# A matmul with rotary embedding: all input tiles turned by TensorE as 32-bit words, in place of fp16 transposes and block pairs

## The chip, the core and the metric

The kernel runs on one core of a Trainium2 chip. The metric is the device time in microseconds of one execution, as the median of several runs. The engines are TensorE (PE; its weight loads are listed apart as PEld), VectorE (DVE), ScalarE (ACT), GpSimd (POOL) and SyncE (SP). Transfers are issued from the queues of SP, ACT and POOL and are moved by the core's 16 DMA engines.

## The reference

```python
batch, seq, hidden, n_heads = (16, 512, 768, 12)      # head_dim 64
y = np.matmul(x, weight)                               # x (16, 512, 768), weight (768, 768), fp32
y = y.reshape(batch, seq, n_heads, head_dim)
y1, y2 = y[..., :head_dim // 2], y[..., head_dim // 2:]
...
out1 = y1 * cos1 - y2 * sin1                           # cos, sin (seq, head_dim), halves 1 and 2
out2 = y2 * cos2 + y1 * sin2
out = np.concatenate([out1, out2], axis=-1).reshape(batch, seq, hidden).astype(np.float32)
```

Every row of x is multiplied by the weight, and in the product each head's two halves are rotated with cos and sin of the row's place in its sequence.

## The kernel before

The 8192 rows of x are cut into 64 tiles of 128 rows (`NTILE`), and four tiles make a group (`QB = 4`, 16 groups, `LAST` is 15). A group holds the same quarter of the sequence rows of four batches, so that one slice of cos and sin serves the whole group.

The contraction runs over 768 values of a row. TensorE needs them on partitions, so each tile has to be transposed. The contraction is split in six chunks (`CHUNKS`, a pair t of 0 to 2 and e of 0 or 1): chunk (t, e) holds the values p·6 + 2t + e for partition p. Two neighbouring fp16 values (e = 0 and 1) form one 32-bit word.

**Plain tiles** (44 of 64) go through four steps. `load` (L188) brings 128 rows of fp32 into one of ten buffers `xs`, issued by SP. `cast` (L223) makes fp16 of them on ACT and sorts them by t, m, e into `xc`. `turn` (L231) lets TensorE transpose the six chunks by an fp16 identity (L238) into the PSUM buffer `pt`, one of two. A copy (L240, run through the helper at L172) moves `pt` to `xt`, on DVE for the first two tiles and on ACT for the rest.

**Block pairs** (20 tiles in ten pairs, the second half of each group from 5 to 14) are transposed by no TensorE instruction. `load_quarter` (L196) brings a quarter of the contraction of two tiles onto 32 partitions; four such transfers make a pair. For odd groups SP issues them in fp32 (`xb`) and ACT casts the pair (`cast_pair`, L243, into `xd`). For even groups POOL issues them and they arrive in fp16 (`xh`). `turn_pair` (L251) then lets DVE transpose 32x32 blocks of 32-bit words into `xp` (L263), in which the two values of a word are neighbours; the matmuls read them with a step of two.

**Matmuls.** `mm_piece` (L297) multiplies one chunk of a tile by the weight (`w_sb`, fp16) into a piece of a PSUM ring `py` of six banks. A tile's 768 output columns fall into two pieces, 512 and 256 wide, so that a tile takes twelve matmuls. The turned x is the stationary operand, the weight the moving one.

**After the matmul.** `rope` (L310) takes 1024 columns at once (a unit; smaller ones in the last two groups): DVE multiplies them by cos and by the signed sin into `tq` (L320), and POOL adds the two products into `ov` (L331); the last four adds are on DVE. `store` (L342) writes half a group of rows, mostly from ACT's queue.

**Order.** Each engine runs its instructions in the order in which the program names them; `Flow.do` adds the waits. After the matmuls of tile i the main loop (L522) names the block transposes up to tile i + 6 (`bturns`, `B_AHEAD`), the plain transposes and evictions up to tile i + 3 (`turns`, `T_AHEAD`), the casts up to tile i + 7 (`casts`, `C_AHEAD`; fewer in the first groups), POOL's loads up to 20 tiles ahead (`pool_loads`) and, at the first and third tile of a group, a store of the group before. `pump` names SP's loads in an order made beforehand (`fetch`, L374), as far as the buffers allow: ten `xs` and three `xb`. Before the loop stands an opening, in which the first four tiles are multiplied chunk by chunk as the weight's six parts arrive (`load_w`, `cast_w`, `mm0`), after twelve matmuls on zeros (`warm`).

Of the kernel before, what the change touches and what calls it, by code (L numbers as in the profile page):

```python
# [103 lines left out]
def kernel(  # L104
# [16 lines left out]
    NH = int(n_heads)  # L121
    D = H // NH
    HD = D // 2
    R = 32
    NQ = P // R
    NT = H // (2 * P)
    SB = S // P
    QB = 4
# [3 lines left out]
    LAST = NG - 1  # L132


    BLOCKS = {}
    for g in range(5, 15):
        BLOCKS[g, 1] = "pool" if g % 2 == 0 and g >= 4 else "sp"

    def sbuf(name, shape, dt):
        return nc.alloc_sbuf_tensor(name, shape, dt).ap()  # L140

    NX, NB, NBH, NC, NCP, NXT, NXP, NTQ, NOV = 10, 3, 3, 5, 2, 8, 4, 3, 4

    ident = sbuf("ident", [P, P], FP16)
    cold = sbuf("cold", [P, 512], FP16)
    sin_sb = sbuf("sin_sb", [P, SB, D], FP32)
    csn = sbuf("csn", [P, 2, SB, D], FP32)
    w_raw = sbuf("w_raw", [P, NT, 2, H], FP32)
    w_sb = sbuf("w_sb", [P, NT, 2, H], FP16)
    xs_b = [sbuf(f"xs{i}", [P, H], FP32) for i in range(NX)]  # L150
    xb_b = [sbuf(f"xb{i}", [P, 2 * H], FP32) for i in range(NB)]
    xh_b = [sbuf(f"xh{i}", [P, 2 * H], FP16) for i in range(NBH)]
    xc_b = [sbuf(f"xc{i}", [P, H], FP16) for i in range(NC)]
    xd_b = [sbuf(f"xd{i}", [P, 2 * H], FP16) for i in range(NCP)]
    xt_b = [sbuf(f"xt{i}", [P, NT, 2, P], FP16) for i in range(NXT)]
    xp_b = [sbuf(f"xp{i}", [P, 2 * H], FP16) for i in range(NXP)]
    tq_b = [sbuf(f"tq{i}", [P, 2, 1024], FP32) for i in range(NTQ)]
    w_flat = w_raw.rearrange("p t e n -> p (t e n)")
    tq_b += [w_flat[:, ts(i, 2048)].rearrange("p (j n) -> p j n", j=2) for i in range(2)]
# [5 lines left out]
    def ring(name, n, state={}):  # L165
        k = state.get((id(f), name), 0)
        state[id(f), name] = k + 1
        return k % n

    def copy(e, o, i_):  # L170
        return lambda eng: (
            eng.copy(out=o, in_=i_) if e == "act" else eng.tensor_copy(out=o, in_=i_)  # L172
        )

    def where(i):
        g, s = divmod(i, QB)
        return QB * (g // SB) + s, g % SB

    def pair_of(i):
        return i // QB, (i % QB) // 2  # L180

    def is_block(i):
        return pair_of(i) in BLOCKS

    xs, xc, xT = {}, {}, {}


    def load(i, e="sp"):  # L188
# [3 lines left out]
        do(e, lambda eng: eng.dma_start(  # L192
            out=xs_b[k], in_=x[b].rearrange("(p r) h -> r p h", r=SB)[r]),
            writes=[f"xs{k}"], dma=f"xs{k}")

    def load_quarter(gh, q):  # L196
        g, h = gh
        b, r = where(g * QB + 2 * h)
        e = BLOCKS[gh]
        src = x[b : b + 2].rearrange("b (j a r) (q k) -> r q a (b j) k", r=SB, a=R, q=NQ)  # L200
        if q == 0:
            xs[gh] = ring("xh", NBH) if e == "pool" else ring("xb", NB)
        k = xs[gh]
        name = f"xh{k}" if e == "pool" else f"xb{k}"
        buf = xh_b[k] if e == "pool" else xb_b[k]
        dst = buf.rearrange("p (j k) -> p j k", j=2 * NQ)
        do(e, lambda eng: eng.dma_start(out=dst[ts(q, R)], in_=src[r, q]),  # L207
           writes=[f"{name}q{q}"], dma=name)

    wv = weight.rearrange("(p t e) n -> t e p n", t=NT, e=2)  # L210

# [19 lines left out]
    def turn(i, e):  # L231
        c = xc[i]
        k = ring("pt", 2)
        z = ring("xt", NXT)
        src = xc_b[c].rearrange("p (t m e) -> p t e m", t=NT, e=2)
        pt = pt_b[k].bitcast(FP16)[:, 0:H].rearrange("p (t e m) -> p t e m", t=NT, e=2)
        for t, h in CHUNKS:
            do("pe", lambda eng: eng.transpose(pt[:, t, h, :], src[:, t, h, :], ident),  # L238
               reads=[f"xc{c}", "ident"], writes=[f"pt{k}"], tick=(t, h) == CHUNKS[-1])
        do(e, copy(e, xt_b[z], pt), reads=[f"pt{k}"], writes=[f"xt{z}"])  # L240
        xT[i] = (lambda t, h: xt_b[z][:, t, h, :], f"xt{z}")

    def cast_pair(gh, e="act"):  # L243
        k = xs[gh]
        c = ring("xd", NCP)
        xc[gh] = c
        do(e, copy(e, xd_b[c].rearrange("p (t j e) -> p t j e", t=NT, e=2),
                   xb_b[k].rearrange("p (j t e) -> p t j e", t=NT, e=2)),
           reads=[f"xb{k}q{q}" for q in range(NQ)], writes=[f"xd{c}"])

    def turn_pair(gh):  # L251
        g, h = gh
        z = ring("xp", NXP)
        dst = xp_b[z].bitcast(FP32)
        if BLOCKS[gh] == "pool":
            k = xs[gh]
            src = xh_b[k].bitcast(FP32).rearrange("p (j t) -> p t j", t=NT)
            rd = [f"xh{k}q{q}" for q in range(NQ)]
        else:
            c = xc[gh]  # L260
            src, rd = xd_b[c].bitcast(FP32), [f"xd{c}"]
        v = xp_b[z].rearrange("p (t m e) -> p t e m", t=NT, e=2)
        do("dve", lambda eng: eng.transpose(out=dst, in_=src), reads=rd, writes=[f"xp{z}"])  # L263
        for s in (0, 1):
            xT[g * QB + 2 * h + s] = (
                lambda t, e, s=s: v[:, t, e, ts(s, P)], f"xp{z}")

    def units(g):  # L270
        if g < LAST - 1:
# [99 lines left out]
        out=sin_sb, in_=sin.rearrange("(p r) d -> p r d", r=SB)), writes=["sin"], dma="sin")  # L371


    fetch, quarters = [], []  # L374
    soon = [p for p in sorted(BLOCKS) if BLOCKS[p] == "sp"]
    for i in range(QB, NTILE):
        if soon and i >= max(2, soon[0][0] - 1) * QB:
            quarters += [(soon[0], q) for q in (0, 2, 1, 3)]
            soon.pop(0)
        if not is_block(i):  # L380
            fetch.append(i)
            if quarters:
                fetch.append(quarters.pop(0))
        elif quarters and quarters[0][0] == pair_of(i):
            fetch.append(quarters.pop(0))
    fetched = [0]
    xs_used, xb_used = [0], [0]
    xs_sent, xb_sent = [4], [0]

    def pump():  # L390

        while fetched[0] < len(fetch):
            j = fetch[fetched[0]]
            if isinstance(j, int):
                if xs_sent[0] - xs_used[0] >= NX:
                    return
                load(j)
                xs_sent[0] += 1
            else:
                if j[1] == 0:  # L400
                    if xb_sent[0] - xb_used[0] >= NB:
                        return
                    xb_sent[0] += 1
                load_quarter(*j)
            fetched[0] += 1

    WARM = 12
    warmed = [0]
# [42 lines left out]
    for c in CHUNKS[3:5]:  # L451
# [6 lines left out]
    do("dve", lambda eng: eng.tensor_scalar_mul(  # L458
        out=csn[:, 1, :, HD:D], in0=sin_sb[:, :, 0:HD], scalar1=-1.0),
        reads=["sin", "csn1", "cos"], writes=["csn"])  # L460
    assert not quarters
    pump()

    state = {"cast": 4, "turn": 4, "bturn": 0, "pool": 0}
    pairs = sorted(BLOCKS)
    pool_pairs = [p for p in pairs if BLOCKS[p] == "pool"]

    def casts(upto):
        while state["cast"] < min(upto, NTILE):
            i = state["cast"]  # L470
            state["cast"] += 1
            if not is_block(i):
                castx(i, "act")
            elif i % 2 == 0 and BLOCKS[pair_of(i)] == "sp":
                cast_pair(pair_of(i))
                xb_used[0] += 1
            pump()

    def turns(upto):
        while state["turn"] < min(upto, NTILE):  # L480
            i = state["turn"]
            state["turn"] += 1
            if not is_block(i):
                turn(i, "act")

    def bturns(upto):
        while state["bturn"] < len(pairs):
            gh = pairs[state["bturn"]]
            if gh[0] * QB + 2 * gh[1] >= upto:
                return  # L490
            turn_pair(gh)
            state["bturn"] += 1

    def pool_loads(upto):
        while state["pool"] < len(pool_pairs):
            gh = pool_pairs[state["pool"]]
            if gh[0] * QB + 2 * gh[1] >= upto:
                return
            for q in (0, 2, 1, 3):
                load_quarter(gh, q)  # L500
            state["pool"] += 1

    C_AHEAD, T_AHEAD, B_AHEAD, P_AHEAD = 7, 3, 6, 20
    SETTLED = 2 * QB


# [15 lines left out]
    for i in range(QB, NTILE):  # L522
        g, s = divmod(i, QB)
        us = units(g)
        done_to = (s + 1) * H
        for p in pieces(g, s):
            a, z, _, bank = p
            for c in CHUNKS:
                mm_piece(i, p, c, c == CHUNKS[0], c == CHUNKS[-1],
                         tick=c == CHUNKS[-1])  # L530
            for u in us:
                if u[1] == z:
                    rope(g, u)
        bturns(i + (B_AHEAD if i >= SETTLED else 3))
        turns(i + 1 + (T_AHEAD if i > QB + 1 else 2))
        casts(i + 1 + (C_AHEAD if i >= SETTLED else 3 if i == QB else 4))
        pool_loads(i + P_AHEAD)
        if s == 0 and g > 0:
            store(g - 1, 0, 2 * H, "act")
        if s == 2 and g > 0:  # L540
            store(g - 1, 2 * H, 4 * H, "act")
        if g == LAST:
            if s == 2:
                store(g, 0, H, "sp")
            if s == 3:
                store(g, H, 2 * H, "act")
# [42 lines left out]
```

## Time and profile before

| | |
|---|---|
| Median of 3 runs | 157.07 us (156.81 to 157.47) |
| Profiled execution, its own time | 156.38 us |
| Its span, first to last instruction | 154.6 us |
| Granted TensorE clock, mean | 0.991 |
| PE / DVE / ACT / POOL busy | 145.2 / 125.8 / 77.4 / 123.4 us |
| Matmuls of tiles (L302) | 768 to py (528 from xt, 240 from xp) and 12 to pt |
| TensorE transposes (L238) | 264 |
| DVE block transposes (L263) | 10, of 1246 ns (from xh) and 968 ns (from xd) |
| ACT casts of tiles / of pairs | 44 of 905 ns / 5 of 1603 ns |
| ACT evictions pt to xt | 42 of 800 ns |
| x transfers to landing, median | 16.2 us (xs), 16.5 us (xb), 12.3 us (xh) |
| Bytes moved, packets under 2 KB | 51.16 MB, 13072 of 27548 packets |

The page shows one profiled execution. A group of instructions is given by its line, engine and operation, the tile it writes and the one it reads, the shape, the count, the busy time and the mean duration of one. TensorE's instructions are pipelined: 264 transposes of 219 ns keep it busy for only 21.9 us, so the step from one to the next, and not the duration, says what one costs. Slices are fortieths of the span, 3.9 us each, and their digits are busy tenths. The chain is followed back from the last instruction through whatever released each step.

### The profile page before, as it was taken

To read this page: it belongs to the slowest core of one execution; us is meant where nothing else is said; L and a number is where in the kernel's file an instruction comes from. 1 tells how busy PE (TensorE), PEld (TensorE's weight loads), DVE (VectorE), ACT (ScalarE), POOL (GpSimd) and SP (SyncE) were. 2 spreads that over 40 slices of the span, in tenths; PEclk is the share of its full clock that TensorE was granted. 3 is DMA by queue.
4 is the path that set the end of the run, shared out by engine and by line. 5 is a ranking of instruction groups with operands and counts; after the bars stand their busy time and mean duration, and the time that the engine had idled before them with its cause. 6 is when DMAs were issued, how large, how long until landed. Compare 5 with 4: busy or idle time off the path is not lost.

```text
span 154.6 us, 2609 instructions
## 1 busy us (share of the span) xinstructions
PE 145.2 (94%) x1056; PEld 91.9 (59%) x1056; DVE 125.8 (81%) x82; ACT 77.4 (50%) x92; POOL 123.4 (80%) x79
## 2 busy tenths in 40 slices
PE   6799999999999999999999999999999999999930
PEld 2345566666666666566666666665666666666720
DVE  0436997688777979998999899898999899997990
ACT  3462959699658615744282707452483418243000
POOL 1000599799888999799989999899988886999940
PEclk9999999999999999999999999999999999999996
DMA  4999999999999999999999999999999963443983
GB/s 138 387 408 397 403 399 401 368 342 362 372 344 302 395 350 336 358 381 363 351 332 385 391 347 318 365 405 368 368 368 360 382 251 139 155 179 150 374 336 106
DMA packets 27548, 51.16 MB, mean 331 GB/s; under 512 B 7184, under 2 KB 13072, under 8 KB 27536
## 3 DMA queue, kind: packets, MB, share of 16 engines
q1 hardware_dynamic: 13504, 24.78, 45.7%
q10 hardware_dynamic: 8592, 24.25, 39.9%
q0 software_dynamic: 5440, 1.97, 10.3%
q8 instruction: 8, 0.13, 0.3%
q14 instruction: 4, 0.03, 0.1%
HBM read 27.79 MB, written 25.17 MB: 343 GB/s over the span
## 4 chain that ended last, share of the span: by engine, by line
PE 84%; DVE 4%; DMA 4%; ACT 2%; SPq 1%; issue 1%; DVEq 0%
PE py L302 76%; PE pt L238 9%; DMA w_raw<-in_weight_dram 4%; DVE xs L320 1%; ACT xc L172 1%; DVE tq L320 1%; DVE ov L331 1%; SPq L192 1%; DVE w_raw L320 1%; SPq L214 1%; ACT xt L172 1%; DVE w_sb L172 0%; DVEq L55 0%; SPq L584 0%; SPq L114 0%
## 5 line engine op out<-in xcount | busy, mean ns | idle before, releaser
L302 PE MATMUL py<-w_sb,xt 128*128 128x256 f16 (+1 forms) x528 | 89.9, 323 | 1.4 <-DVE w_sb L172 1.1
L331 POOL TENSOR_TENSOR ov<-tq 128x1024 f32<-128x1024 f32 (+2 forms) x33 | 68.9, 2105 | 21.6 <-DVE tq L320 21.4
L320 DVE TENSOR_TENSOR tq<-py,csn 128x2048 f32<-128x2048 f32 (+2 forms) x33 | 66.4, 2024 | 9.3 <-PE py L302 8.9
L302 PEld LDWEIGHTS py<-w_sb,xt 128*128 128x128 f16 x528 | 50.3, 98 | 32.6 <-DVE w_sb L172 2.8
L172 ACT COPY xt<-pt 128x768 f16<-128x768 f16 x42 | 33.5, 800 | 56.1 <-PE pt L238 56.1
L320 DVE TENSOR_TENSOR w_raw<-py,csn 128x2048 f32<-128x2048 f32 (+1 forms) x20 | 41.4, 2068 | 5.8 <-PE py L302 5.7
L331 POOL TENSOR_TENSOR ov<-w_raw 128x1024 f32<-128x1024 f32 (+1 forms) x20 | 42.8, 2149 | 2.6 <-DVE w_raw L320 2.6
L172 ACT CAST xc<-xs 128x768 f16<-128x768 f32 x44 | 39.2, 905 | 8.6 <-DMA xs<-in_x_dram 8.4
L302 PE MATMUL py<-w_sb,xp 128*128 128x512 f16 (+1 forms) x240 | 42.3, 326 | 0.0
L302 PEld LDWEIGHTS py<-w_sb,xp 128*128 128x128 f16 x240 | 22.6, 98 | 12.9
L238 PE MATMUL pt<-ident,xc 128*128 128x128 f16 x264 | 21.9, 219 | 0.2 <-ACT xc L172 0.2
L238 PEld LDWEIGHTS pt<-ident,xc 128*128 128x128 f16 x264 | 18.0, 98 | 6.8 <-ACT xc L172 2.0
L207 POOL DMA_DIRECT2D xh<-in_x_dram x20 | 11.7, 590 | 0.0
L172 ACT CAST xd<-xb 128x1536 f16<-128x1536 f32 x5 | 8.0, 1603 | 0.0
L263 DVE STREAM_TRANSPOSE xp<-xh 128x768 f32<-128x768 f32 x5 | 6.2, 1246 | 0.0
L172 DVE CAST w_sb<-w_raw 128x768 f16<-128x768 f32 x6 | 3.4, 559 | 3.5 <-DMA w_raw<-in_weight_dram 3.5
L413 PE MATMUL py<-cold 128*128 128x512 f16 x12 | 4.6, 552 | 1.4 <-DVE cold L356 1.4
L172 DVE COPY xt<-pt 128x768 f16<-128x768 f16 x2 | 1.1, 558 | 4.8 <-PE pt L238 4.8
L263 DVE STREAM_TRANSPOSE xp<-xd 128x768 f32<-128x768 f32 x5 | 4.8, 968 | 0.0
L413 PEld LDWEIGHTS py<-cold 128*128 128x128 f16 x12 | 1.4, 131 | 3.4 <-issue 1.9
L172 ACT ACT_TABLE_LOAD x1 | 1.3, 1283 | 0.9 <-SPq L114 0.9
L302 PE MATMUL pt<-w_sb,xt 128*128 128x256 f16 x12 | 1.5, 272 | 0.0
(13 smaller groups left out, 6.8 us busy)
## 6 DMA issues: line engine op xcount, KB each, us to landing
out_dram<-ov ACTq DMA_DIRECT2D x30, 768.0 KB, 8.3
xs<-in_x_dram SPq DMA_DIRECT2D x44, 384.0 KB, 16.2
xb<-in_x_dram SPq DMA_DIRECT2D x20, 192.0 KB, 16.5
w_raw<-in_weight_dram SPq DMA_DIRECT2D x6, 384.0 KB, 6.7
xh<-in_x_dram POOLq DMA_DIRECT2D x20, 96.0 KB, 12.3
out_dram<-ov SPq DMA_DIRECT2D x1, 384.0 KB, 2.8
out_dram<-ov ACTq DMA_DIRECT2D x1, 384.0 KB, 2.5
out_dram<-ov SPq DMA_DIRECT2D x1, 256.0 KB, 2.0
```

The source lines that it names most:

```text
L172: eng.copy(out=o, in_=i_) if e == "act" else eng.tensor_copy(out=o, in_=i_)
L192: do(e, lambda eng: eng.dma_start(out=xs_b[k], in_=x[b].rearrange("(p r) h -> r p h", r=SB)[r]), writes=[f"xs{k}"], dma=f"xs{k}")
L207: do(e, lambda eng: eng.dma_start(out=dst[ts(q, R)], in_=src[r, q]), writes=[f"{name}q{q}"], dma=name)
L214: do(e, lambda eng: eng.dma_start(out=w_raw[:, t, h], in_=wv[t, h]), writes=[f"wr{t}{h}"], dma=f"w{t}{h}")
L238: do("pe", lambda eng: eng.transpose(pt[:, t, h, :], src[:, t, h, :], ident), reads=[f"xc{c}", "ident"], writes=[f"pt{k}"], tick=(t, h) == ...
L263: do("dve", lambda eng: eng.transpose(out=dst, in_=src), reads=rd, writes=[f"xp{z}"])
L302: do("pe", lambda eng: eng.matmul(ps, get(t, h), w_sb[:, t, h, a - s * H : z - s * H], start=start, stop=stop), reads=[key, f"w{t}{h}"], w ...
L320: do("dve", lambda eng: eng.tensor_tensor(out=tq.rearrange("p j (h d) -> p j h d", d=D), in0=ps.rearrange("p (h d) -> p h d", d=D) .unsque ...
L331: do(adder, lambda eng: eng.tensor_tensor(out=ov_b[o][:, ds(c0, w)].rearrange("p (h t d) -> p h t d", t=2, d=HD), in0=tq[:, 0].rearrange(" ...
L413: do("pe", lambda eng: eng.matmul(py[:, ts(b, 512)], cold[:, 0:P], cold, start=True, stop=warmed[0] < WARM - 6), reads=["cold"], writes=[f ...
```

## The change

The block pairs go, with their buffers (`xb`, `xh`, `xd`, `xp`), their transfers, casts and DVE transposes. All 64 tiles take the way of a plain tile. In `turn`, TensorE transposes the fp16 tile as fp32 words, three 128x128 transposes per tile in place of six, with an fp32 identity; the copy out of PSUM still moves 768 fp16 values, and the matmuls read them with a step of two. The freed space goes to buffers: 18 `xs` in place of 10, 6 `xc` for 5, 4 `tq` for 3. Casts run five tiles ahead instead of seven.

```diff
-    BLOCKS = {}
-    for g in range(5, 15):
-        BLOCKS[g, 1] = "pool" if g % 2 == 0 and g >= 4 else "sp"
...
-    NX, NB, NBH, NC, NCP, NXT, NXP, NTQ, NOV = 10, 3, 3, 5, 2, 8, 4, 3, 4
-
-    ident = sbuf("ident", [P, P], FP16)
+    NX, NC, NXT, NTQ, NOV = 18, 6, 8, 4, 4
+
+    ident = sbuf("ident", [P, P], FP32)
...
-    xt_b = [sbuf(f"xt{i}", [P, NT, 2, P], FP16) for i in range(NXT)]
-    xp_b = [sbuf(f"xp{i}", [P, 2 * H], FP16) for i in range(NXP)]
+    xt_b = [sbuf(f"xt{i}", [P, H], FP16) for i in range(NXT)]
...
-        src = xc_b[c].rearrange("p (t m e) -> p t e m", t=NT, e=2)
-        pt = pt_b[k].bitcast(FP16)[:, 0:H].rearrange("p (t e m) -> p t e m", t=NT, e=2)
-        for t, h in CHUNKS:
-            do("pe", lambda eng: eng.transpose(pt[:, t, h, :], src[:, t, h, :], ident),
-               reads=[f"xc{c}", "ident"], writes=[f"pt{k}"], tick=(t, h) == CHUNKS[-1])
-        do(e, copy(e, xt_b[z], pt), reads=[f"pt{k}"], writes=[f"xt{z}"])
-        xT[i] = (lambda t, h: xt_b[z][:, t, h, :], f"xt{z}")
...
+        src = xc_b[c].bitcast(FP32)
+        pt = pt_b[k][:, 0 : H // 2]
+        for t in range(NT):
+            do("pe", lambda eng: eng.transpose(pt[:, ts(t, P)], src[:, ts(t, P)], ident),
+               reads=[f"xc{c}", "ident"], writes=[f"pt{k}"], tick=t == NT - 1)
+        do(e, copy(e, xt_b[z], pt.bitcast(FP16)), reads=[f"pt{k}"], writes=[f"xt{z}"])
+        v = xt_b[z].rearrange("p (t m e) -> p t e m", t=NT, e=2)
+        xT[i] = (lambda t, h: v[:, t, h, :], f"xt{z}")
...
-    fetch, quarters = [], []
...
+    sent, xs_used = [4], [0]
 
     def pump():
...
+        while sent[0] < NTILE and sent[0] - xs_used[0] < NX:
+            load(sent[0])
+            sent[0] += 1
...
     def casts(upto):
         while state["cast"] < min(upto, NTILE):
-            i = state["cast"]
+            castx(state["cast"], "act")
             state["cast"] += 1
-            if not is_block(i):
-                castx(i, "act")
-            elif i % 2 == 0 and BLOCKS[pair_of(i)] == "sp":
-                cast_pair(pair_of(i))
-                xb_used[0] += 1
             pump()
...
-    C_AHEAD, T_AHEAD, B_AHEAD, P_AHEAD = 7, 3, 6, 20
+    C_AHEAD, T_AHEAD = 5, 3
...
-        bturns(i + (B_AHEAD if i >= SETTLED else 3))
         turns(i + 1 + (T_AHEAD if i > QB + 1 else 2))
         casts(i + 1 + (C_AHEAD if i >= SETTLED else 3 if i == QB else 4))
-        pool_loads(i + P_AHEAD)
```

Cut out are the functions `load_quarter`, `cast_pair`, `turn_pair`, `bturns`, `pool_loads`, `pair_of` and `is_block`, which go, and the book-keeping of the old `pump`.

More of the change, by code (lines that the diff above doesn't have):

```diff
@@ L123 @@
     HD = D // 2
-    R = 32
-    NQ = P // R
     NT = H // (2 * P)
@@ L150 @@
     xs_b = [sbuf(f"xs{i}", [P, H], FP32) for i in range(NX)]
-    xb_b = [sbuf(f"xb{i}", [P, 2 * H], FP32) for i in range(NB)]
-    xh_b = [sbuf(f"xh{i}", [P, 2 * H], FP16) for i in range(NBH)]
     xc_b = [sbuf(f"xc{i}", [P, H], FP16) for i in range(NC)]
-    xd_b = [sbuf(f"xd{i}", [P, 2 * H], FP16) for i in range(NCP)]
-    xt_b = [sbuf(f"xt{i}", [P, NT, 2, P], FP16) for i in range(NXT)]
-    xp_b = [sbuf(f"xp{i}", [P, 2 * H], FP16) for i in range(NXP)]
+    xt_b = [sbuf(f"xt{i}", [P, H], FP16) for i in range(NXT)]
     tq_b = [sbuf(f"tq{i}", [P, 2, 1024], FP32) for i in range(NTQ)]
@@ L177, in where @@
         return QB * (g // SB) + s, g % SB
[L179 to L183, printed above, removed]
     xs, xc, xT = {}, {}, {}
@@ L194, in load @@
             writes=[f"xs{k}"], dma=f"xs{k}")
[L196 to L208, printed above, removed]
     wv = weight.rearrange("(p t e) n -> t e p n", t=NT, e=2)
@@ L234, in turn @@
         z = ring("xt", NXT)
-        src = xc_b[c].rearrange("p (t m e) -> p t e m", t=NT, e=2)
-        pt = pt_b[k].bitcast(FP16)[:, 0:H].rearrange("p (t e m) -> p t e m", t=NT, e=2)
-        for t, h in CHUNKS:
-            do("pe", lambda eng: eng.transpose(pt[:, t, h, :], src[:, t, h, :], ident),
-               reads=[f"xc{c}", "ident"], writes=[f"pt{k}"], tick=(t, h) == CHUNKS[-1])
-        do(e, copy(e, xt_b[z], pt), reads=[f"pt{k}"], writes=[f"xt{z}"])
-        xT[i] = (lambda t, h: xt_b[z][:, t, h, :], f"xt{z}")
[L243 to L266, printed above, removed]
+        src = xc_b[c].bitcast(FP32)
[6 more added lines that the diff above has]
+        xT[i] = (lambda t, h: v[:, t, h, :], f"xt{z}")
     def units(g):
@@ L371 @@
         out=sin_sb, in_=sin.rearrange("(p r) d -> p r d", r=SB)), writes=["sin"], dma="sin")
-    fetch, quarters = [], []
[L375 to L379, printed above, removed]
-        if not is_block(i):
[L381 to L388, printed above, removed]
-    def pump():
[L392 to L405, printed above, removed]
+    sent, xs_used = [4], [0]
+    def pump():
+        while sent[0] < NTILE and sent[0] - xs_used[0] < NX:
+            load(sent[0])
+            sent[0] += 1
     WARM = 12
@@ L460 @@
         reads=["sin", "csn1", "cos"], writes=["csn"])
-    assert not quarters
     pump()
-    state = {"cast": 4, "turn": 4, "bturn": 0, "pool": 0}
-    pairs = sorted(BLOCKS)
-    pool_pairs = [p for p in pairs if BLOCKS[p] == "pool"]
+    state = {"cast": 4, "turn": 4}
     def casts(upto):
         while state["cast"] < min(upto, NTILE):
-            i = state["cast"]
+            castx(state["cast"], "act")
             state["cast"] += 1
-            if not is_block(i):
-                castx(i, "act")
-            elif i % 2 == 0 and BLOCKS[pair_of(i)] == "sp":
-                cast_pair(pair_of(i))
-                xb_used[0] += 1
             pump()
@@ L480, in turns @@
         while state["turn"] < min(upto, NTILE):
-            i = state["turn"]
+            turn(state["turn"], "act")
             state["turn"] += 1
[L483 to L501, printed above, removed]
-    C_AHEAD, T_AHEAD, B_AHEAD, P_AHEAD = 7, 3, 6, 20
+    C_AHEAD, T_AHEAD = 5, 3
     SETTLED = 2 * QB
```

## The prediction

> **What bounds the kernel now.** I read the page's engine shares first, then its slices, then the chain that ended last (its shares on the page, and its pieces in order of time), and last the groups of instructions and the waits for what stands beside the chain.
>
> ```profile
> PE 145.2 (94%) x1056; PEld 91.9 (59%) x1056; DVE 125.8 (81%) x82; ACT 77.4 (50%) x92; POOL 123.4 (80%) x79
> ...
> PE   6799999999999999999999999999999999999930
> ...
> PEclk9999999999999999999999999999999999999996
> DMA  4999999999999999999999999999999963443983
> ```
>
> TensorE is busy in every slice from the third to the last but two, at the full granted clock. The DMA row is equally full until about 120 us, so one has to know which of the two sets the pace. The chain settles it:
>
> ```profile
> PE py L302 76%; PE pt L238 9%; DMA w_raw<-in_weight_dram 4%; DVE xs L320 1%; ACT xc L172 1%; DVE tq L320 1%; DVE ov L331 1%; SPq L192 1%; DVE w_raw L320 1%; SPq L214 1%; ACT xt L172 1%; DVE w_sb L172 0%; DVEq L55 0%; SPq L584 0%; SPq L114 0%
> ```
>
> The x transfers are not on it. TensorE's matmuls (L302) and transposes (L238) are 85% of it, and the weight's arrival stands at its start. In order of time, between 30 and 70 us, it is a metronome:
>
> ```profile
> 50.71 1.95 PE py L302 x12
> 52.66 0.34 PE pt L238 x6
> 53.00 5.85 PE py L302 x36
> 58.85 0.34 PE pt L238 x6
> 59.18 1.95 PE py L302 x12
> 61.13 0.34 PE pt L238 x6
> 61.47 5.85 PE py L302 x36
> 67.32 0.34 PE pt L238 x6
> 67.65 1.95 PE py L302 x12
> ```
>
> One tile's matmuls take 1.95 us (12 instructions; 5.85 for three tiles). A plain tile's six fp16 transposes add 0.335 us, 55.8 ns each. A group of four plain tiles, as in the windows of 25 to 53 us, takes 9.14 us; a group with a block pair, 59.18 to 67.65, takes 8.47 us, because its two pair tiles need no transposes on TensorE. So the quantity that decides this change is the step from one TensorE transpose to the next.
>
> **The change, part by part.** *Transposes of plain tiles.* 44 tiles are plain. The first three are turned while TensorE still waits for weights (cast_w, up to about 10 us), so 41 lie on the path: 41 × 0.335 = 13.7 us, which agrees with the chain's 9% of 154.6 us. After the change 61 tiles lie on the path, each with three transposes of 32-bit words; with T for the step of one, they cost 183 × T. The change on TensorE's path is 183 T − 13.7 us, and it breaks even at T = 75 ns.
>
> *T is not in the trace:* no TensorE row has a 32-bit operand. These rows bound it:
>
> ```profile
> L238 PE MATMUL pt<-ident,xc 128*128 128x128 f16 x264 | 21.9, 219 | 0.2 <-ACT xc L172 0.2
> L238 PEld LDWEIGHTS pt<-ident,xc 128*128 128x128 f16 x264 | 18.0, 98 | 6.8 <-ACT xc L172 2.0 <-issue 0.7
> ```
>
> The low end is 56 ns. A transpose then still streams 128 columns and its step follows the columns, as everything on TensorE does here: 4608 matmul columns of a tile in 1.95 us is 0.423 ns a column, or 54 ns for 128, and a transpose steps at 55.8. Then 183 × 0.0558 = 10.2 us, a gain of 3.5 us. I exclude anything below: nothing in the trace streams a column faster. The middle value is 112 ns, if the step follows the bytes: 20.5 us, a loss of 6.8 us. The high end is 219 ns, the duration of one transpose in the row above, if the load and the pass of 32-bit words did not overlap with their neighbours (or took four passes, 223 ns): 40.1 us, a loss of 26.4 us. I take 56 ns. The nearest sign in the trace of what 32-bit data do is that the 128x768 casts of w_sb from fp32 take DVE 559 ns and the copies xt of the same shape from fp16 558 ns: elements count there, not bytes. That is another engine, so all three stay in.
>
> Two rules of the Trainium skill pull on T in opposite ways. The page "TensorE: Matmul & The Clock Gate", section "Terms", says that trn2's transpose mode makes an fp32 transpose four times faster; no row here has one. By it T would be one pass, and the sum would be the low end. The same page, section "Weight-path perf modes — Fast Weight Load (FWL) and DoubleRow", says that the fast weight load does not apply to fp32, and its section "LDWEIGHTS (loading the stationary operand)" puts an ordinary load at columns divided by 1.2 GHz, 107 ns for 128. This speaks against the change: the row above shows loads of 98 ns with a step of 56, so fp16 loads hide behind the passes, and a load that blocks for 107 ns would make T 107 and the sum a loss of 5.9 us (an estimate from that page).
>
> *Matmuls.* Their number and shapes stay. Their stationary operand is now read with a step of two elements for all tiles (xt with m before e), as it was from xp for pair tiles: the loads take 98 ns from xp and 98 ns from xt, and the pair tiles' matmuls keep the 1.95 us. Nothing.
>
> *ScalarE.* It loses 5 pair casts (8.0 us) and gains 20 casts of 905 ns and 20 evictions of 800 ns, 34.1 us: 77.4 + 26.1 = 103.5 us busy, about 67%. Neighbouring instructions overlap a little: back to back, a copy and a cast of one tile step by 1.49 us (34.07 to 35.56 us in the timeline), so a group needs 6.0 us of ACT out of TensorE's 8.47. The evictions come three tiles ahead of their matmuls as before; the casts move from seven to five ahead. What hides this is the 2.5 us of idle ACT per group; if it were gone, ACT's order (evict, cast, store issue) would set the pace. The store issues (0.38 us each, two per group) sit on ACT's own queue and wait for POOL's adds, and the next eviction is behind them. The adds have 11.7 us less of DMA issuing (20 × 590 ns) beside them on POOL, so they come no later. Nothing. Evictions still move 768 fp16 values from PSUM, the same row of 800 ns.
>
> *VectorE and GpSimd.* DVE loses ten block transposes (6.2 + 4.8 us), POOL the twenty DMA issues. Neither is worth time: TensorE has no wait on a DVE read of py in the list of waits, and in pair groups DVE does 7.6 to 7.9 us of work in 8.47. In the groups that gain, DVE needs three multiplies of 2.28 us (6.84) and POOL three adds of 2.37 (7.1) in a group that shrinks from 9.14 to 8.47 us. This is the pace that pair groups have already, with more work on both. The fourth tq buffer only adds slack. The identity in fp32 costs POOL some 0.5 us near 1.3 us, needed at 5.2 us. Nothing.
>
> *The x transfers.* 40 small transfers (20 of 192 KB on SP, 20 of 96 KB on POOL's queue) become 20 of 384 KB on SP, which still issues 64 transfers; counted bytes go from 51.16 to about 53.1 MB, and the packets under 2 KB largely disappear. At 8.47 us per group the steady need is 4 × 2 × 0.393 MB = 3.15 MB, or 371 GB/s. The trace moves 402 GB/s from 10 to 20 us, 354 to 361 in the windows that follow, and 368 on average in slices 2 to 31. The need stands slightly above that, but loads finish near 120 us now while the last cast starts at 131.6, after which the DMA row falls to 3 to 6 tenths. Eighteen buffers let SP run 18 tiles ahead instead of 10 (SP waited 22.9 us on casts to free a buffer). I price it at zero, hidden by that lead. If the lead ran out, 3.15 MB at 361 GB/s takes 8.71 us, 0.24 us per group over 14 groups, 3.4 us.
>
> *The ends.* Until 10 us weights set the time; from the last matmul to the end DVE's and POOL's adds and the stores set it, all unchanged.
>
> **Sum.** The profiled execution took 156.38 us, 1.8 us outside its span of 154.6. With T = 56 ns: 154.6 − 3.5 = 151.1, plus 1.8 is 152.9. That execution was 0.7 us below the median of the runs (157.07), so the forecast on that scale is 153.6 us.
>
> **Rivals.** First, 32-bit words cost TensorE by the byte or by a load that no longer hides: T near 112 ns (100 to 130), 157.07 + 6.8 = 163.8 us. It decides from T = 75 ns on, and its place is L238 on TensorE. For it: every operand here is 16 bits wide, and loads take 98 ns, longer than the step, so they must already be hidden. Against it: the step now equals the columns' time, with no sign of a load in it. Second, serial or fourfold transposes, T near 219 ns: 157.07 + 26.4 = 183.5 us. Third, TensorE has the gain but transfers cannot follow: up to 3.4 us are given back, near 157 us. For it: the need of 371 against 354 to 361 GB/s, x transfers that take 16.2 us to land, and one 1.6 us wait of ACT for one at 43 us. Against it: the large packets and the lead.
>
> **How the numbers follow.** T near 56 ns, 153.6 us (own range 152.2 to 155.5, up to T = 66 ns): 0.50. By bytes or load, 163.8 us: 0.27. Fourfold, 183.5 us: 0.15. Transfers, 157 us: 0.08. The first case is all faster; the last is mostly no change. About 0.5% (0.8 us) is what a measurement of this kernel can tell from none, so faster 0.51, same 0.06, slower 0.43. The range runs from 152.2 to 165.0 us: it holds the first case, the transfers and most of the second, and leaves out the fourfold one and the second's upper part, about 0.2.
>
> **What would show it.** Right: in the chain, pieces "PE pt x3" of about 0.17 us between matmuls of 1.95 us, groups of 8.47 us from start to end, PE busy near 141 us, ACT near 103 us, no DVE block transposes. Pieces of 0.34 us or 0.66 us mean the first or second rival. Waits of ACT xc for x transfers past 30 us, followed by idle TensorE, mean the third. The forecast is wrong if T exceeds 66 ns, or if changing between 16-bit and 32-bit operands costs TensorE more than about 30 ns a tile (61 × 0.03 = 1.8 us).

## The result and the profile after

The changed kernel takes 163.15 us (median of 4 runs, 162.95 to 163.40) against 156.94 us for the kernel before on the same chip. The ratio is 1.0397, with a 95% interval of 1.0376 to 1.0418: it is 4% slower. (Ratios leave out executions over 1.5% above the fastest of their kernel; only one run below, with block pairs in groups 3 to 15, had such ones, five of twelve.) The profiled execution has a span of 161.6 us, 7.0 us more than before.

The engine shares of the page, after:

```profile
PE 151.7 (94%) x984; PEld 99.0 (61%) x984; DVE 116.8 (72%) x72; ACT 102.1 (63%) x127; POOL 112.8 (70%) x59
...
DMA  4999999999999999999999999996555433344883
...
PE py L246 72%; PE pt L208 12%; DMA w_raw<-in_weight_dram 4%; DVE xs L264 1%; DVE tq L264 1%; ACT xc L162 1%; DVE ov L275 1%; SPq L176 1%; SPq L184 1%; ACT xt L162 0%; DVE w_raw L264 0%; DVE w_sb L162 0%; DVEq L55 0%; SPq L473 0%; SPq L114 0%
```

TensorE is as full as before (94%), DVE and POOL have become idler by 9 to 11 us each, and the time is longer all the same: the work that left DVE and POOL had not been on the path, and the work that came stands on it. In the last line the share of the transposes (now L208) has grown from 9% to 12% of a longer span. Pieces of the chain in order of time (start us, length us), after:

```profile
55.57 0.33 PE pt L208 x3
55.90 1.95 PE py L246 x12
57.85 0.33 PE pt L208 x3
58.17 1.95 PE py L246 x12
```

A tile's matmuls still take 1.95 us, but three transposes of 32-bit words take 0.33 us, as long as six fp16 ones. Each steps by 109 ns. The metronome of before let two of four tiles of a group pass without transposes (5.85 us for three tiles); now every tile carries its 0.33. The two groups of instructions behind the transposes, after:

```profile
L208 PE MATMUL pt<-ident,xc 128*128 128x128 f32 x192 | 31.7, 274 | 0.7 <-ACT xc L162 0.7
L208 PEld LDWEIGHTS pt<-ident,xc 128*128 128x128 f32 x192 | 23.5, 141 | 8.7 <-ACT xc L162 2.7 <-issue 0.7
```

One transpose lasts 274 ns where the fp16 one lasted 219, and that is also what an fp16 matmul of 256 columns lasts in the same profile (273 ns); the ends of passes are modelled in the profile, so the step from start to start is the firmer number. One load lasts 141 ns where the fp16 one lasted 98. So two theories were open: 128 columns of 32-bit words stream at half rate (stream theory), or their load, which has become longer, no longer hides behind a pass and sets the step (load theory).

### The profile page after: what moved, and what is told of

It is laid out like the page before. It is cut to its first block, busy times and chain, and to the rows that moved or that the text cites. A ratio compares the mean times of both kernels' runs of the same rounds, so it can differ in the third digit from the quotient of the medians.

```text
span 161.6 us, 2444 instructions
## 1 busy us (share of the span) xinstructions
PE 151.7 (94%) x984; PEld 99.0 (61%) x984; DVE 116.8 (72%) x72; ACT 102.1 (63%) x127; POOL 112.8 (70%) x59
## 2 busy tenths in 40 slices
DMA packets 19547, 53.11 MB, mean 329 GB/s; under 512 B 1744, under 2 KB 2512, under 8 KB 19536
## 4 chain that ended last, share of the span: by engine, by line
PE 85%; DMA 4%; DVE 4%; ACT 2%; SPq 1%; issue 1%; DVEq 0%
PE py L246 72%; PE pt L208 12%; DMA w_raw<-in_weight_dram 4%; DVE xs L264 1%; DVE tq L264 1%; ACT xc L162 1%; DVE ov L275 1%; SPq L176 1%; SPq L184 1%; ACT xt L162 0%; DVE w_raw L264 0%; DVE w_sb L162 0%; DVEq L55 0%; SPq L473 0%; SPq L114 0%
## 5 line engine op out<-in xcount | busy, mean ns | idle before, releaser
L246 PE MATMUL py<-w_sb,xt 128*128 128x256 f16 (+1 forms) x768 | 133.9, 324 | 1.3 <-DVE w_sb L162 1.1
L246 PEld LDWEIGHTS py<-w_sb,xt 128*128 128x128 f16 x768 | 74.7, 98 | 43.7 <-DVE w_sb L162 2.8
L275 POOL TENSOR_TENSOR ov<-tq 128x1024 f32<-128x1024 f32 (+2 forms) x36 | 75.8, 2116 | 33.8 <-DVE tq L264 33.8
L264 DVE TENSOR_TENSOR tq<-py,csn 128x2048 f32<-128x2048 f32 (+2 forms) x36 | 72.9, 2038 | 20.1 <-PE py L246 19.9
L162 ACT COPY xt<-pt 128x768 f16<-128x768 f16 x62 | 49.4, 798 | 39.8 <-PE pt L208 39.8
L162 ACT CAST xc<-xs 128x768 f16<-128x768 f32 x64 | 57.6, 904 | 7.3 <-DMA xs<-in_x_dram 7.2
L264 DVE TENSOR_TENSOR w_raw<-py,csn 128x2048 f32<-128x2048 f32 (+2 forms) x17 | 35.2, 2072 | 10.3 <-PE py L246 10.1
L275 POOL TENSOR_TENSOR ov<-w_raw 128x1024 f32<-128x1024 f32 (+2 forms) x17 | 36.5, 2148 | 7.9 <-DVE w_raw L264 7.9
L208 PE MATMUL pt<-ident,xc 128*128 128x128 f32 x192 | 31.7, 274 | 0.7 <-ACT xc L162 0.7
L208 PEld LDWEIGHTS pt<-ident,xc 128*128 128x128 f32 x192 | 23.5, 141 | 8.7 <-ACT xc L162 2.7
```

The costliest lines, as they stand in the source:

```text
L208: do("pe", lambda eng: eng.transpose(pt[:, ts(t, P)], src[:, ts(t, P)], ident), reads=[f"xc{c}", "ident"], writes=[f"pt{k}"], tick=t == NT ...
L246: do("pe", lambda eng: eng.matmul(ps, get(t, h), w_sb[:, t, h, a - s * H : z - s * H], start=start, stop=stop), reads=[key, f"w{t}{h}"], w ...
L264: do("dve", lambda eng: eng.tensor_tensor(out=tq.rearrange("p j (h d) -> p j h d", d=D), in0=ps.rearrange("p (h d) -> p h d", d=D) .unsque ...
L275: do(adder, lambda eng: eng.tensor_tensor(out=ov_b[o][:, ds(c0, w)].rearrange("p (h t d) -> p h t d", t=2, d=HD), in0=tq[:, 0].rearrange(" ...
```

## Experiments

Each run is compared with the kernel before on the same chip.

**Half the load.**

```diff
-            do("pe", lambda eng: eng.transpose(pt[:, ts(t, P)], src[:, ts(t, P)], ident),
+            do("pe", lambda eng: eng.transpose(pt[0:64, ts(t, P)], src[:, t * P : t * P + 64], ident),
...
+    for k in range(2):
+        do("dve", lambda eng: eng.memset(pt_b[k], 0.0), writes=[f"pt{k}"])
```

(the clearing of pt runs once, at the start)

> The changed kernel, each of its three transposes loading only 64 of the 128 word columns (the other half of each tile is left unturned and reads as zeros). Two theories of why a 32-bit transpose steps by 109 ns where an fp16 one steps by 56. Stream theory: the 128 columns of the moving identity pass at half the rate of 16-bit columns, so the step depends on the moving columns alone. It expects pieces of 0.33 us for three transposes as before and 163.2 us. Load theory: the load of 128 columns of 32-bit words takes about 107 ns and cannot hide behind a pass of 54 ns. It expects half a load, a step of about 56 ns, pieces of 0.17 us and 163.2 - 183 x 0.053 = 153.5 us.

Measured: 163.32 us, ratio 1.0409 (1.0375 to 1.0444). A part of its chain:

```profile
57.95 0.33 PE pt L208 x3
58.28 1.95 PE py L246 x12
```

And its loads, in the view of the tile (count, then the shortest, median and longest duration in ns):

```profile
L208 PEld LDWEIGHTS pt<-ident,xc x192: 108/111/177, 5.2 to 149.0; 128*64 128x64 f32 x192
```

The load is shorter by 30 ns (median 111 ns against 141) and the three transposes still take 0.33 us: the step did not follow the load. That speaks against the load theory, but 111 ns is still about one step, so this run alone doesn't close the case; the next two do.

**Half the moving columns.**

```diff
-            do("pe", lambda eng: eng.transpose(pt[:, ts(t, P)], src[:, ts(t, P)], ident),
+            do("pe", lambda eng: eng.transpose(
+                pt[:, t * P : t * P + 64], src[0:64, ts(t, P)], ident[0:64, 0:64]),
```

(with the same clearing of pt at the start)

> The changed kernel, each of its three transposes taking 64 of the 128 partitions, against a 64x64 identity (the other half of the rows is left unturned and reads as zeros). The load still has 128 columns, the pass only 64. Stream theory: the step halves to about 55 ns, pieces of 0.17 us, 163.2 - 9.8 = 153.4 us. Load theory: the step stays at 109 ns, 163.2 us.

Measured: 169.21 us, ratio 1.0800 (1.0756 to 1.0845). Neither theory gives that. The edit halves the moving columns and, with them, the partitions of load and pass. The timeline of weight loads (start us, length us), first of the changed kernel, then of this run, shows the steps:

```profile
62.13 0.36 PEld L208 LDWEIGHTS pt<-ident,xc 128*128 128x128 f32 x3
...
60.04 0.26 PEld L208 LDWEIGHTS pt<-ident,xc 64*128 64x128 f32 x3 [0.21 <-issue]
60.37 1.63 PEld L247 LDWEIGHTS py<-w_sb,xt 128*128 128x128 f16 x12
```

And this run's passes, and pieces of its chain:

```profile
60.04 0.40 PE L208 MATMUL pt<-ident,xc 64*128 64x64 f32 x3
60.37 2.12 PE L247 MATMUL py<-w_sb,xt 128*128 128x256 f16 x12
...
55.34 0.33 PE pt L208 x3
55.67 2.06 PE py L247 x12
```

Three loads of 138 ns each fit in 0.26 us, so they step by 0.06 us (0.26 − 0.138 is two steps); in the changed kernel three loads of 141 ns take 0.36 us, a step of 0.11. The passes themselves start 0.11 and then 0.06 us apart; the record of the first is 50 ns longer than the other two (272 ns against 222), as it begins together with its own load. So the step halved, as the stream theory says, and a load of 138 ns stood beside a step of 62 ns, so the load's length doesn't set the step. That the columns halved it, and not the partitions that were halved with them, is not separated here.

The run is slower because the edit changed something else: TensorE falls idle where transposes on 64 of 128 partitions meet their full neighbours. In the stretch shown the last full matmul before them starts 0.20 us ahead of the first transpose, where a matmul of its width steps by 0.11; and from the third transpose to the next full matmul 0.15 us pass. The twelve matmuls keep their length (2.12 us here, 2.11 in the changed kernel's timeline). The chain's pieces, which run to the start of the next instruction on the chain, hide this: 0.33 us here is three short steps and a gap, and 2.06 us is the 1.95 us of before and a gap. It isn't a wait for the tile's data: the cast of the tile shown had ended 2.7 us before its transposes. The period of a tile is 2.38 us instead of 2.28, and 61 × 0.10 = 6 us is the difference between the two runs. The expected time missed this side of the edit; the step is what bears on the theories.

**Transposes spread between matmuls.**

```diff
+    def turn(i, e, between=None):
...
         for t in range(NT):
+            if between:
+                between(t)
             do("pe", lambda eng: eng.transpose(pt[:, ts(t, P)], src[:, ts(t, P)], ident),
...
+        if i > QB + 1 and state["turn"] < NTILE:
+            turn(state["turn"], "act", lambda t: matmuls((t + 1) * n // 4))
+            state["turn"] += 1
+        matmuls(n)
```

> The changed kernel with the three transposes of a tile spread between the matmuls of another tile, one after each quarter of them, from the seventh tile on; all of the work is done. Load theory: a load of 107 ns then hides behind a matmul of 109 or 216 ns, so each transpose costs only its pass of about 56 ns: 163.2 - 9.6 = 153.6 us, faster than both kernels. Stream theory: a pass costs 109 ns wherever it stands: 163.2 us, within 0.5 us.

Measured: 167.71 us, ratio 1.0698 (1.0668 to 1.0728). Its chain between 55 and 60 us:

```profile
55.14 0.11 PE pt L210
55.25 1.29 PE py L248 x6
56.55 0.11 PE pt L210
56.66 0.65 PE py L248 x3
...
59.70 0.11 PE pt L210
```

And its windows of 20 to 50 us, then the first of them in the changed kernel (the length of the window, then PE's busy time):

```profile
20.00:30.00 10.00, 7.60 (x54) 5.17 (x53) 6.91 (x4) 6.45 (x9) 8.84 (x5) 1.00 1.03 405
30.00:50.00 20.00, 18.60 (x122) 12.20 (x121) 13.22 (x6) 13.20 (x17) 12.76 (x6) 1.00 1.03 414
...
20.00:30.00 10.00, 9.77 (x66) 6.40 (x65) 8.31 (x4) 7.65 (x10) 9.57 (x5) 1.00 1.03 406
```

Beside a matmul that steps by 216 ns a load of 141 ns fits whole, and a lone transpose still costs 0.11 us there, as it does beside one of 109 ns. This, with the two runs before, rules the load theory out. Once the kernel runs steadily two tiles take 4.56 us (55.14 to 59.70 us), the same as two tiles of 2.28 us in the changed kernel. That is what the stream theory expects, and spreading gains nothing. The expected time was missed: most of the 4.6 us that this run's span is longer are lost near the opening. TensorE is idle for 3.8 us between 20 and 50 us, where the changed kernel idles for 0.2. There the chain passes through ACT's casts and evictions: a transpose named early waits for a cast that is not done, and the matmuls behind it on TensorE wait with it (waits of TensorE's transposes for casts: 4.2 us in this run, 0.7 in the changed kernel).

**Six fp16 transposes, no block pairs.**

```diff
-        src = xc_b[c].bitcast(FP32)
...
+        for t, h in CHUNKS:
+            do("pe", lambda eng: eng.transpose(pt[:, t, h, :], src[:, t, h, :], ident),
```

> The changed kernel with six fp16 transposes per tile in place of three of 32-bit words; still no block pairs, still 18 input buffers. Both theories of the step: 0.335 us per tile against 0.328, 61 x 0.007 = 0.4 us more, 163.6 us. That would mean that the 32-bit words gained almost nothing and the whole loss comes from the 20 pair tiles, which now pass through TensorE. A rival: the larger buffers or the packets cost something by themselves and the 32-bit words hide it; then this run would differ from 163.2 by more than 1 us.

Measured: 164.05 us, ratio 1.0463 (1.0434 to 1.0492); its span is 162.0 us, 0.4 more than with 32-bit words, and its median 0.9 us more. Its chain:

```profile
53.28 0.34 PE pt L208 x6
53.61 1.95 PE py L246 x12
```

Without the block pairs the kernel is slow with either kind of transpose.

**32-bit words, block pairs kept.** The change to `turn` and `ident` alone, in the kernel before.

> The kernel before, with all its block pairs and buffers, and the 44 plain tiles turned as three 32-bit words in place of six fp16 values. If a transpose costs by its bytes (three steps of 109 ns against six of 55.8, as the changed kernel shows), it gains 41 x 0.007 = 0.3 us, no change that can be told: 156.4 to 156.9 us. A rival: turning 32-bit words among block pairs costs more, by the switch of operand width; then it is slower by over 1 us.

Measured: 157.07 us, ratio 0.9996 (0.9981 to 1.0011), no difference. Chain:

```profile
52.91 0.33 PE pt L238 x3
53.24 5.85 PE py L303 x36
59.09 0.33 PE pt L238 x3
```

These two runs and the two kernels make a square: the loss of the pairs costs 4 to 4.6% with either kind of transpose, and the words change nothing that can be told beside the pairs and gain 0.4 us (span) to 0.9 us (median) without them.

**The old buffers.**

```diff
-    NX, NC, NXT, NTQ, NOV = 18, 6, 8, 4, 4
+    NX, NC, NXT, NTQ, NOV = 10, 5, 8, 3, 4
-    C_AHEAD, T_AHEAD = 5, 3
+    C_AHEAD, T_AHEAD = 7, 3
```

> The changed kernel with the buffer counts and the lead of before: 10 input buffers for 18, 5 xc for 6, 3 tq for 4, casts seven tiles ahead. If TensorE alone sets the pace and the buffers are worth nothing, 163.2 us within 0.5. If the 18 buffers carry the transfers at the higher need, x arrives late and TensorE idles: 164 to 166 us. If the deeper queue of x transfers is what delays the opening (0.65 us later than before in the two profiles), 162.5 us.

Measured: 163.09 us, ratio 1.0376 (1.0353 to 1.0400), as with 18 buffers. Their number has no part in the result, and the third tile's cast starts as late as with 18 (8.29 us against 8.25).

**More block pairs.** If TensorE's path is all that counts, the way is the opposite of the change. One more pair, in group 15, in the kernel before:

```diff
-    for g in range(5, 15):
+    for g in range(5, 16):
```

> The kernel before with one block pair more, in the last group (15). If TensorE's path is what counts, two tiles fewer to turn, 0.67 us less: about 156.1 us, if DVE, which has shorter multiplies but also the last adds there, hides one more block transpose. If DVE or the arrival of the pair is late, no change or slower.

Measured: 156.19 us, ratio 0.9928 (0.9904 to 0.9951): faster than both kernels, by 0.9 us against the kernel before, where 0.67 was expected. With `range(3, 16)`:

> The kernel before with block pairs in groups 3 to 15 in place of 5 to 14, 26 pair tiles. TensorE turns six tiles fewer, 2.0 us less: about 154.7 us, faster than both kernels. A rival: the pairs of groups 3 and 4 are loaded while the first tiles still arrive, in small packets, so x is late for the early tiles and TensorE idles: 157 us or slower.

Measured: ratio 0.9946 (0.9917 to 0.9975). The twelve executions spread from 155.18 to 162.72 us, and the median of all of them, 157.08 us, is that of the kernel before (157.12). So a gain is not certain, and it isn't the 2 us. From its chain:

```profile
16.00 0.43 SPq L207
16.43 0.04 issue
16.48 16.29 DMA xs<-in_x_dram
32.77 0.02 issue
32.79 0.90 ACT xc L172
```

SP issues the early pairs' quarters between the first tiles' loads. The 13th plain tile is issued at 16.48 us and lands at 32.77; in the kernel before it was issued at 10.98 and landed at 24.36. TensorE waits for its cast. The rate falls to 227 and 228 GB/s in the slices from 19 to 27 us, where the kernel before moved 399 and 401. The mechanism is that of the rival that was written down for this run; whether the rate fell because of the quarters' small packets or of their place in the order is not separated.

**Words and one pair more.** The 32-bit words with `range(5, 16)`:

> The kernel before with one block pair more, in group 15, and 32-bit words for its 42 plain tiles: the one part of the change that costs nothing joined to the edit that goes the other way. If both act on TensorE's path alone and add up: 39 plain tiles on the path at 0.328 us against 41 at 0.335, 0.9 us less than before, about 156.1 us.

Measured: 156.10 us, ratio 0.9930 (0.9908 to 0.9952). And with `range(4, 16)`:

> The same with a block pair in group 4 too, 24 pair tiles: 37 plain tiles on the path at 0.328 us, 1.6 us less than before, about 155.5 us, if it is the pair of group 3 alone whose loading starved the early tiles when groups 3 to 15 had pairs. If the pair of group 4 starves them as well, TensorE idles near 30 us and the time is above that of the run with group 15 alone.

Measured: 156.05 us, ratio 0.9921 (0.9895 to 0.9947). Its chain runs at 2.28 us per tile from 26 to 45 us without a gap, so the pair of group 4 starves nothing. The time doesn't show the 0.67 us that it should add over group 15 alone, but the two traces do: from the seventh tile's matmuls to those behind the last transposes, 111.22 us (26.29 to 137.51) against 111.88 (25.92 to 137.80). In the execution with 24 pair tiles it is lost outside this stretch: these matmuls start 0.37 us later, and from the last multiplies and adds to the end of the span 0.7 us more pass.

## Why the prediction was wrong

The frame held and one term failed. *T*, the step of a 32-bit transpose, was taken as 56 ns, because the pass "still streams 128 columns and its step follows the columns"; it is 109 ns, as long as a pass of 256 columns of fp16. Put into the prediction's own sum, 183 × 0.1092 − 13.7 = 6.2 us, hence 154.6 + 6.2 + 1.8 + 0.7 = 163.3 us against the measured 163.15. The first rival (by bytes, 112 ns, 163.8 us) had that value, and the range reached to it, but the greater chance stood on the wrong side. Of this rival's two mechanisms the runs leave the bytes and rule out the load.

The reason for 56 ns was a pair of DVE rows: fp32 and fp16 operands at the same 559 and 558 ns. A row of another engine says nothing about TensorE's moving operand. The trace before held no TensorE row with 32-bit operands, and the prediction said so; no row of TensorE spoke for 56 ns over 112.

Of the two rules weighed, neither gave the number. The Trainium skill, "TensorE: Matmul & The Clock Gate", section "Terms", has the transpose mode four times faster for fp32; the prediction read it as one pass at 16-bit speed, and the runs show one step of 109 ns, half the four passes of 223 ns. No plain fp32 matmul was run here, so the factor itself stays untested. The same page's sections on weight loads put an ordinary load of 128 columns at 107 ns and keep the fast one from fp32. The records have 141 ns, against 98 for fp16 and 111 for half the columns (an estimate from these two: 60 ns for 128 columns and a fixed part), and half the load left the step where it was: the 32-bit load is longer than the fp16 one, but it hides.

The rest, by its steps:

- *TensorE's path.* Right: from 26 us on a constant period, no waits for x or for DVE in it. The span's 7.0 us are 6.2 us from the transposes, 0.65 us from an opening in which the third tile arrived later (its cast starts at 8.25 us against 7.59), and a small rest. Whether the change delays that arrival stays open: the cast starts between 8.22 and 8.55 us in all six profiles without block pairs and between 7.48 and 8.20 in all six with them, but no run looked for a cause. Between the medians lie 6.2 us, what the transposes alone make up, so that the sum above comes out within 0.2 us is in part luck.
- *Matmuls with a step of two.* Right: 98 ns a load, 1.95 us a tile.
- *ScalarE.* Right: 102.1 us busy against 103.5 worked out, and hidden.
- *VectorE and GpSimd.* Right: both idler, worth nothing.
- *The x transfers.* Right at zero. The window of 25 to 53 us of the kernel before; the last number is GB/s:

```profile
25.00:53.00 28.00, 27.93 (x224) 18.61 (x225) 21.20 (x11) 21.79 (x28) 25.12 (x18) 1.00 1.08 356
```

The same window of the changed kernel:

```profile
25.00:53.00 28.00, 27.77 (x184) 18.35 (x183) 20.52 (x10) 21.22 (x27) 22.00 (x10) 1.00 1.03 414
```

The plain rows move at 414 GB/s, well over the 371 that the third rival asked for; it took the rate of before (354 to 361) for a limit. The last x lands at 110.4 us instead of 122.3, and TensorE gains nothing from it.

## What to carry to other kernels

On a path that one engine fills, count what an edit adds to that engine and not the work that it takes from the others; here 6.6 us of transposes (20 × 0.33) were moved from engines with room onto the one without. Where the deciding price has no row of its own engine and operand width in the trace, keep both bounds at like chances, or measure that one step first: a small kernel with that one operation could have shown the 109 ns here. An experiment that narrows one operand can change how neighbours overlap, so read the step in the records and not only the total.

## What the hardware showed beyond that

- In transposes TensorE streams 128 columns of 32-bit words in the time of 256 fp16 columns (109 ns), so that 32-bit words move no more bytes per microsecond than 16-bit ones: 0.33 against 0.335 us for a tile.
- Three transposes on 64 of the 128 partitions between full matmuls cost TensorE about 0.25 us beyond their steps (2.38 us a tile, less 1.95 of matmuls and three steps of 0.06): it falls idle before them and after them.
- Whole rows of 3 KB were moved at up to 414 to 419 GB/s (2512 packets under 2 KB), where the kernel before, with 13072 such packets, moved 356 between 25 and 53 us. With ten buffers, as before, whole rows still moved 414 in that window, so the buffers aren't the reason; that the packets are wasn't tested by itself.
